# Transposes of the copied probabilities asked for two units later in each step, and the norm's power behind the normalisations on GpSimd

## The chip, the cores and the metric

The kernel runs on one core of one Trainium2 chip. A core has TensorE (PE, which loads its weights through a queue of its own, PEld), VectorE (DVE), ScalarE (ACT), GpSimd (POOL) and SyncE (SP, which here only issues transfers). Each engine works through its own queue in order; semaphores tell an engine that another one is done. The metric is the time of one launch in microseconds of device time, as the median of several runs. A profile is one further execution, recorded by the hardware profiler.

## What is computed

One layer of a hybrid backbone over 2048 latent tokens of width 1024, with 256 context tokens, all in fp32. From the reference, cut:

```python
h  = rms_norm(x) * (1 + scale) + shift
rq, rk, rv, rg, aq, ak, av, ag = project(h, w_in)
# group A: retention, 4 heads of 128, chunks of 128, forward and backward
y  = inner + cross                       # per chunk: (q k^T * decay) v, and q R * decay
y  = (y - mu) * rsqrt(var + EPS)         # per head
ret_x = y * gn_w * silu(rg)
# group B: attention, 8 heads of 64 (2 key heads), window +-128, 256 context keys, a sink
p  = exp(logits - m); p = p / (sum(p) + exp(sink - m))
att_x = (p[..., :Lc] @ v_ctx + p[..., Lc:] @ v_window) * silu(ag)
x  = x + gate * (concat(ret_x, att_x) @ w_out)
out = rms_norm(x) * final_norm_w
```

Products that must be near fp32 are made as three products of a high and a low part in fp32r (a x b high, high x low, low x high: `PASSES`).

## The kernel before

The first stage (to about 690 us in the profile) makes the normalised input and all its projections and puts queries, keys, values, gates and retention states in DRAM. The second stage, which the change concerns, works through 16 blocks of 128 tokens. A block b has two **steps**: t = 2b (kv = 0, an even step) and t = 2b + 1 (kv = 1, an odd step), one for each key head with its four query heads. Heads are prepared one step ahead: while step t multiplies probabilities with values, it makes the scores and probabilities for step t + 1.

What a step does is written as a row of **units**, in `STEPS[kv]`. A letter is a kind of work, the digit a part of it (the digits of a table's row and those of a tile's name are not the same):

- `a0`..`a3`: scores S of one head for the next step (four matmuls into the one PSUM tile S, L753 and L757), then VectorE adds the mask and takes the maximum (L759) and ScalarE takes the exponential (L768).
- `N0`..`N3`: the head's probabilities are normalised on GpSimd (L778, `p<-p`), then SP copies them (L782, `pr<-p`) into a second SBUF tile, from which TensorE may read them as fp32r.
- `T0`..`T4`: four transposes of the copied probabilities of one key tile (L1209, `pt<-identr,pr`), one for each head, into a PSUM bank; ScalarE takes the high part out (L1211, `phl`), VectorE the low part (L1212, `phl`).
- `V0`..`V4`: two matmuls with the values (L1222, `o`), one on the high and one on the low part.
- `o0`..`o7`: three matmuls each of the output projection (L1259, `pz`); `O`: the attention output of the step before (ACT `ob`, VectorE `mf`, GpSimd `ma`).
- Retention: `q` (decayed queries on GpSimd, L798, `qd`), `S` (scores `s`), `R` (the twelve products `y`, L813 to L815, and ScalarE's copy of them to `sd`), `B` (moments on VectorE), `r2` (the norm: GpSimd adds EPS and raises to -0.5, L119 and L120, `ra`; VectorE L832), `r0`, `r1` (two rows each of `sd` scaled on ScalarE, L839), `Y` (transposes `yt`; VectorE `gr` L1245; GpSimd `mr` L111 and L1248), `U` (VectorE's update of the state, L847, `st`, and the loads for the next blocks).
- `f`, `F0`, `F1`: the final norm of a finished block.

PSUM banks are short: S has one, `o` one, `pz` two, and `pt`, `y`, `s` and `yt` share three. The three `p` tiles in use rotate over all heads, and the copies of `phl` are two deep.

The row is what the kernel asks for. The framework that records the kernel then writes each engine's queue, and pulls an instruction ahead of others where it reckons with a wait. `with behind(i)` fixes that what stands inside comes after instruction i on its engine; the helper takes None for no such bond. The dictionary `PE` holds such instructions: `PE["norm"]` is the last normalisation recorded (L778), `PE["phl"]` the last high part. The retention norm has no such bond before the change; `qd` (L798) and the rows of `r0`, `r1` have one.

## Time and profile before

| what | us |
|---|---|
| median of 3 runs (lowest, highest) | 1181.89 (1181.22, 1182.31) |
| the profiled execution, its own time | 1180.44 |
| its span | 1178.7 |
| TensorE busy in the span | 1132.1 |
| first stage, 0 to 690: TensorE busy | 680.8 |
| second stage, one block in the middle | 30.0 |

The profiled execution lies 1.45 us below the median and 1.74 us above its own span. In a timeline a line gives the start, the length, the engine, the line of the code, the operation with output and inputs (without the buffers' numbers), the shapes, how many in a row, and in brackets the engine's idle time before it with what ended it. "PE busy" counts pipelined matmuls, so that it is nearly all of the time whenever no wait stands between them.

### The profile page before, as it was taken

How to read it: one execution, taken by the hardware profiler on the slowest of the kernel's cores; microseconds unless marked ns; L12 is line 12 of the kernel's file. 1: busy time of each engine (PE TensorE's matmuls, PEld its weight loads, DVE VectorE, ACT ScalarE, POOL GpSimd, SP SyncE). 2: the span in 40 equal slices, each digit the busy share in tenths (PEclk: the TensorE clock that was granted, in tenths of full speed). 3: DMA queues.
4: the chain of work that ended last, by engine and by line, in shares of the span. 5: the costliest groups of instructions: out<-in, count | busy, mean ns of one | idle time of the engine just before them, and what ended most of it. 6: DMA issues, size and time to landing. Idle time of an engine off the chain costs nothing. (4 is left out here: it accounts for less than half of the span.)

```text
span 1178.7 us, 18728 instructions
## 1 busy us (share of the span) xinstructions
PE 1132.1 (96%) x6317; PEld 966.0 (82%) x6318; DVE 796.4 (68%) x2028; ACT 476.7 (40%) x1032; POOL 323.3 (27%) x427
## 2 busy tenths in 40 slices
PE   8999999999999999999999987999999999999997
PEld 5887889999888899998888866788888888888885
DVE  7884974665557366475672656777777777777775
ACT  4445422343342022231111454555555555555553
POOL 0000020101002101011141523544444444455443
PEclk9998999999999999999999988999999999999999
DMA  9949982484575334353382674666666666666531
GB/s 332 348 124 288 297 290 68 152 269 147 177 248 170 90 117 135 94 166 107 90 270 91 188 250 149 223 208 220 210 216 217 217 217 213 214 210 214 181 123 72
DMA packets 158551, 224.38 MB, mean 190 GB/s; under 512 B 13299, under 2 KB 105203, under 8 KB 158326
## 3 DMA queue, kind: packets, MB, share of 16 engines
q1 hardware_dynamic: 143380, 215.54, 55.3%
q10 hardware_dynamic: 15074, 7.64, 2.2%
q8 instruction: 50, 0.82, 0.3%
q14 instruction: 47, 0.39, 0.1%
HBM read 130.19 MB, written 50.86 MB: 154 GB/s over the span
## 5 line engine op out<-in xcount | busy, mean ns | idle before, releaser
L768 ACT ACTIVATE p<-p,m 128x641 f32<-128x641 f32 (+1 forms) x128 | 105.0, 820 | 100.4 <-DVE m L765 55.9
L778 POOL TENSOR_SCALAR p<-p,m 128x640 f32<-128x640 f32 (+1 forms) x128 | 101.3, 795 | 104.5 <-DVE m L777 60.1
L1212 DVE TENSOR_TENSOR phl<-pt,phl 128x512 fp32r<-128x512 f32 x156 | 106.5, 685 | 33.8 <-ACT phl L1211 32.8
L759 DVE CUSTOM_DVE_ANT_0 p<-S,msk 128x640 f32<-128x640 f32 (+1 forms) x128 | 102.6, 802 | 31.5 <-PE S L757 9.4
L1211 ACT ACTIVATE phl<-pt 128x512 fp32r<-128x512 f32 x156 | 91.2, 595 | 65.7 <-PE pt L1209 60.4
L1259 PE MATMUL pz<-wg0h,mr 128*128 128x512 f32 x256 | 100.3, 407 | 1.2 <-DVE mr L115 1.0
L1259 PE MATMUL pz<-wg1h,ma 128*128 128x512 f32 x256 | 100.1, 409 | 0.1
L1209 PEld LDWEIGHTS pt<-identr,pr 128*128 128x128 f32 x624 | 70.1, 141 | 34.5 <-DMA pr<-p 23.0
L1209 PE MATMUL pt<-identr,pr 128*128 128x128 f32 x624 | 76.3, 241 | 22.2 <-DMA pr<-p 20.0
L753 PE MATMUL S<-kwin,aq 128*128 128x384 f32 (+1 forms) x256 | 84.2, 349 | 8.0 <-DVE p L764 5.0
L445 ACT ACTIVATE vw<-v,wdec 128x128 fp32r<-128x128 f32 x128 | 43.7, 394 | 84.3 <-DVE v L458 84.3
L1222 PE MATMUL o<-phl,vwin 128*128 128x512 f32 x184 | 70.7, 445 | 2.0 <-DVE phl L1212 1.5
L757 PE MATMUL S<-kctx,aq 128*128 128x256 f32 x256 | 72.0, 284 | 0.0
L753 PEld LDWEIGHTS S<-kwin,aq 128*128 128x128 f32 x256 | 49.0, 191 | 14.5 <-DVE m L759 6.2
L1259 PEld LDWEIGHTS pz<-wg0h,mr 128*128 128x128 f32 x256 | 48.6, 190 | 11.2 <-DVE mr L115 1.3
L1259 PEld LDWEIGHTS pz<-wg1h,ma 128*128 128x128 f32 x256 | 47.9, 188 | 8.3 <-POOL ma L1237 0.8
L757 PEld LDWEIGHTS S<-kctx,aq 128*128 128x128 f32 x256 | 49.3, 193 | 4.4
L1259 PE MATMUL pz<-wg0l,mr 128*128 128x512 f32 x128 | 51.0, 398 | 0.0
L1259 PE MATMUL pz<-wg1l,ma 128*128 128x512 f32 x128 | 50.4, 393 | 0.0
L1233 DVE TENSOR_TENSOR mf<-o,ob 64x256 f32<-64x256 f32 x64 | 26.5, 414 | 27.0 <-ACT ob L1230 26.3
L447 DVE SCALAR_TENSOR_TENSOR vw<-v,wdec,vw 128x128 fp32r<-128x128 f32 x128 | 40.0, 358 | 6.7 <-ACT vw L445 6.7
L1222 PEld LDWEIGHTS o<-phl,vwin 128*128 128x128 f32 x184 | 33.0, 193 | 12.5 <-ACT phl L1211 4.5
(425 smaller groups left out, 3037.2 us busy)
## 6 DMA issues: line engine op xcount, KB each, us to landing
pr<-p SPq DMA_DIRECT2D x112, 320.0 KB, 3.2
wss<-in_wss SPq DMA_DIRECT2D x32, 512.0 KB, 6.4
qkv<-d_qkv SPq DMA_DIRECT2D x15, 768.0 KB, 7.1
aq<-d_aq SPq DMA_DIRECT2D x64, 128.0 KB, 2.8
xb<-in_xn SPq DMA_DIRECT2D x16, 512.0 KB, 4.9
out<-xb SPq DMA_DIRECT2D x31, 256.0 KB, 2.6
st<-d_st SPq DMA_DIRECT2D x15, 512.0 KB, 3.4
d_g<-g ACTq DMA_DIRECT2D x28, 256.0 KB, 2.8
```

The costliest lines, as they stand in the source:

```text
L445: act.activation(vw[0][:, hh, dr, :], x, AF.Copy, scale=w)
L447: dve.scalar_tensor_tensor(vw[1][:, hh, dr, :], x, w, vw[0][:, hh, dr, :], op0=ALU.mult, op1=ALU.subtract)
L753: i = pe.matmul(psc[:, o:512].rearrange("p (s t) -> p s t", t=P), AQ[b][:, h, :], C2["kwin"][:, kv, hl, ksel], start=(hl == 0), stop=(hl = ...
L757: pe.matmul(psc[:, 512:768], AQ[b][:, h, :], C2["kctx"][:, kv, hl], start=(hl == 0), stop=(hl == 1))
L759: i = dve.tensor_tensor_reduce(out=pb[:, 0:n], in0=psc[:, o : o + n], in1=mk, op0=ALU.add, op1=ALU.max, scale=1.0, scalar=-3e38, accum_out ...
L768: act.activation(pb[:, 0 : n + 1], pb[:, 0 : n + 1], AF.Exp, bias=m4[:, 1, j : j + 1], scale=0.125, accum_out=m4[:, 2, j : j + 1],)
L778: PE["norm"] = pool.tensor_scalar(pb[:, 0:n], pb[:, 0:n], m4[:, 2, j : j + 1], 0.0, op0=ALU.mult, op1=ALU.add)
L1209: pe.transpose(ppt[:, j].bitcast(F32R), pb[:, j, kt * P : (kt + 1) * P], identr)
L1211: PE["phl"] = act.activation(phl[:, 0], ppt, AF.Copy)
L1212: PE["low"] = dve.tensor_tensor(phl[:, 1], ppt, phl[:, 0], op=ALU.subtract)
L1222: pe.matmul(PO[kv], vt, PH[kt][:, hl], start=(kt == 0 and hl == 0), stop=(kt == nkt - 1 and hl == 1))
L1259: pe.matmul(PZ[n2], m[:, a, k % RH, :], WG[k // 4][c][:, k % 4, s], start=(k == 0 and i == 0), stop=(k == NK - 1 and i == 2),)
```

## The change

Three things change. In both rows of `STEPS` the transposes T0 stand two units later (in the even step behind `a1 N0 o2` instead of directly behind `o1`, in the odd step behind `a1 N0 R`), most of the other T and V follow them more closely, and `r2` of the odd step comes behind `N3`. T0 is bound to stand on TensorE behind the last product recorded before it, of the projection or of y. And the norm's sum and power on GpSimd are bound to stand behind the last normalisation recorded.

```diff
 STEPS = (
-    "a0 o0 O o1 T0 r0 a1 N0 T1 r1 o2 V0 U a2 N1 T2 o3 Y V1 o4 a3 N2 T3 o5 V2 q o6 T4 N3 o7 V3 S f V4",
-    "a0 o0 O o1 T0 a1 N0 T1 R F0 F1 V0 a2 N1 T2 B V1 o2 a3 N2 T3 o3 V2 o4 T4 r2 N3 o5 V3 o6 V4 o7",
+    "a0 o0 O o1 a1 N0 o2 T0 r0 T1 r1 U a2 N1 V0 o3 T2 Y V1 o4 a3 N2 T3 V2 o5 q T4 N3 o6 V3 S o7 f V4",
+    "a0 o0 O o1 a1 N0 R T0 F0 F1 a2 N1 T1 B V0 o2 T2 V1 a3 N2 o3 T3 o4 V2 T4 N3 r2 o5 V3 o6 o7 V4",
 )
...
-            pe.matmul(py[:, h], sd[:, h], v[:, h], start=False, stop=True)
+            PE["prod"] = pe.matmul(py[:, h], sd[:, h], v[:, h], start=False, stop=True)
...
-        rs = inv_sqrt(ra[:, 0], mv[:, :, 1], 1)
+        with behind(PE["norm"] if b else None):
+            rs = inv_sqrt(ra[:, 0], mv[:, :, 1], 1)
...
-        for j in range(4):
-            pe.transpose(ppt[:, j].bitcast(F32R), pb[:, j, kt * P : (kt + 1) * P], identr)
+
+        with behind(PE.get("prod") if kt == 0 else None):
+            for j in range(4):
+                pe.transpose(ppt[:, j].bitcast(F32R), pb[:, j, kt * P : (kt + 1) * P], identr)
...
-            pe.matmul(
+            PE["prod"] = pe.matmul(
                 PZ[n2], m[:, a, k % RH, :], WG[k // 4][c][:, k % 4, s],
```

The queues show what this does in the middle blocks. On TensorE, in the odd step of block 7, the names carry block, key head and key tile: `pt7_1_0` is the tile of T0, `S8_1` the scores of the second head for block 8, `y8` the products of block 8. Before:

```order
L1209 MATMUL pt7_1_0_9106<-identr_71,pr7_1_8884 128x128 x3
L753 MATMUL S8_1_9114<-kwin_5977,aq8_8701 128x384
L757 MATMUL S8_1_9114<-kctx_5989,aq8_8701 128x256
L753 MATMUL S8_1_9114<-kwin_5977,aq8_8701 128x384
L757 MATMUL S8_1_9114<-kctx_5989,aq8_8701 128x256
L1209 MATMUL pt7_1_1_9126<-identr_71,pr7_1_8884 128x128 x3
L1209 MATMUL pt7_1_0_9106<-identr_71,pr7_1_8884 128x128
L1209 MATMUL pt7_1_1_9126<-identr_71,pr7_1_8884 128x128
L813 MATMUL y8_9134<-st7_8590,qd8_9022 128x128
```

Now, at the same place, from the end of the second scores on (eleven of the twelve y stand between; the first is ahead of the scores):

```order
L757 MATMUL S8_1_9106<-kctx_5989,aq8_8701 128x256
L814 MATMUL y8_9118<-st8_8952,qd8_9022 128x128
L815 MATMUL y8_9118<-qkv8_8517,sd8_9023 128x128
L813 MATMUL y8_9118<-st7_8587,qd8_9022 128x128
...
L814 MATMUL y8_9118<-st8_8952,qd8_9022 128x128
L815 MATMUL y8_9118<-qkv8_8517,sd8_9023 128x128
L1212 MATMUL pt7_1_0_9132<-identr_71,pr7_1_8884 128x128 x4
L753 MATMUL S8_2_9144<-kwin_5977,aq8_8701 128x384
```

T0, whose fourth transpose needs the copy of the fourth head, has moved from ahead of the products y to behind them.

On GpSimd, in the same odd step: `p8_0_1` to `p8_0_3` are the normalisations of three heads for block 8, `ra8` the norm's sum and power, `ma7` the attention output. Before:

```order
L778 TENSOR_SCALAR p8_0_1_9078<-p8_0_1_9078,m48_0_9076 128x640
L119 TENSOR_SCALAR ra8_9185<-mv8_9176 128x4
L120 TENSOR_TENSOR ra8_9185<-ra8_9185,half4_86 128x4
L778 TENSOR_SCALAR p8_0_2_9079<-p8_0_2_9079,m48_0_9076 128x640
L778 TENSOR_SCALAR p8_0_3_9080<-p8_0_3_9080,m48_0_9076 128x640
```

Now:

```order
L778 TENSOR_SCALAR p8_0_1_9078<-p8_0_1_9078,m48_0_9076 128x640
L778 TENSOR_SCALAR p8_0_2_9079<-p8_0_2_9079,m48_0_9076 128x640
L778 TENSOR_SCALAR p8_0_3_9080<-p8_0_3_9080,m48_0_9076 128x640
L119 TENSOR_SCALAR ra8_9174<-mv8_9165 128x4
L120 TENSOR_TENSOR ra8_9174<-ra8_9174,half4_86 128x4
```

The two instructions of the norm have moved behind both normalisations.

On ScalarE, in the even step of block 8: `phl8_0_0` is the high part of T0's tile, `sd8` two rows of the retention, `p8_1_1` the exponential of the second head. Before:

```order
L768 ACTIVATE p8_1_0_9251,m48_1_9250<-p8_1_0_9251,m48_1_9250 128x641
L1211 ACTIVATE phl8_0_0_9283<-pt8_0_0_9278 128x512
L839 ACTIVATE sd8_9023<-sd8_9023,ra8_9185 128x128 x2
L1211 ACTIVATE phl8_0_1_9305<-pt8_0_1_9300 128x512
L768 ACTIVATE p8_1_1_9252,m48_1_9250<-p8_1_1_9252,m48_1_9250 128x641
L839 ACTIVATE sd8_9023<-sd8_9023,ra8_9185 128x128 x2
L1211 ACTIVATE phl8_0_2_9341<-pt8_0_2_9336 128x512
```

Now:

```order
L768 ACTIVATE p8_1_0_9251,m48_1_9250<-p8_1_0_9251,m48_1_9250 128x641
L1214 ACTIVATE phl8_0_0_9298<-pt8_0_0_9293 128x512
L768 ACTIVATE p8_1_1_9252,m48_1_9250<-p8_1_1_9252,m48_1_9250 128x641
L840 ACTIVATE sd8_9023<-sd8_9023,ra8_9174 128x128 x2
L1214 ACTIVATE phl8_0_1_9308<-pt8_0_1_9303 128x512
L840 ACTIVATE sd8_9023<-sd8_9023,ra8_9174 128x128 x2
L768 ACTIVATE p8_1_2_9253,m48_1_9250<-p8_1_2_9253,m48_1_9250 128x641
L1214 ACTIVATE phl8_0_2_9344<-pt8_0_2_9339 128x512
```

The exponential of the second head has moved from behind the second high part to directly behind the first, and that of the third head ahead of the third high part. The lines of the changed kernel are one higher from L832 on, three higher from L1211 on.

## Prediction

> **What bounds the kernel now.** I read the page first, then the time by stage, then the waits of TensorE, and last the timeline and the chain of one block.

> ```profile
> span 1178.7 us, 18728 instructions
> PE 1132.1 (96%) x6317; PEld 966.0 (82%) x6318; DVE 796.4 (68%) x2028; ACT 476.7 (40%) x1032; POOL 323.3 (27%) x427
> 956.00:986.00 30.00, 28.71 (x179) 24.95 (x178) 23.59 (x76) 17.48 (x37) 15.14 (x20) 1.00 0.63 210
> ```

> The third row is one block of the second stage (columns: stretch, length, then busy time of PE, PEld, DVE, ACT and POOL, the granted clock, the DMA share). PE works 28.71 of 30.00 us, no other engine over 23.6: PE is the bound, and only its idle 1.29 us a block are to be had. The longest of the waits of PE from 690 us on names them (total, times, longest):

> ```profile
> PE pt L1209 <- DMA pr<-p: 20.0, 19, 2.0
> ```

> These 20.0 us are the transposes waiting for the copied probabilities. By place:

> ```profile
> 769.61 0.36 PE L1209 MATMUL pt<-identr,pr 128*128 128x128 f32 x2 [1.28 <-DMA pr<-p]
> 1099.96 0.36 PE L1209 MATMUL pt<-identr,pr 128*128 128x128 f32 x2 [1.30 <-DMA pr<-p]
> 1129.52 0.28 PE L1209 MATMUL pt<-identr,pr 128*128 128x128 f32 x1 [1.96 <-DMA pr<-p]
> 753.77 0.28 PE L1209 MATMUL pt<-identr,pr 128*128 128x128 f32 x1 [0.48 <-DMA pr<-p]
> ```

> The first two are the first and last of 12, one in each odd step, 1.26 to 1.34 us each, 15.4 in all. The third is the last odd step with products behind it. The fourth is the longest of a few small ones in even steps; these and one wait in the first odd step make the remaining 20.0 - 15.4 - 2.0 = 2.6 us. The chain through one of the twelve:

> ```profile
> 970.85 0.62 POOL mr L111
> 972.83 0.80 POOL p L778
> 973.63 2.50 POOL qd L798 x2
> 976.13 0.79 POOL p L778
> 976.94 2.80 DMA pr<-p
> 979.78 0.36 PE pt L1209 x2
> ```

> GpSimd works without a pause from 970.85, the last normalisation stands behind the 2.5 us of `qd`, and its copy lands 2.8 us after that. PE was there 1.29 us before.

> **The transposes of an odd step.** The change puts T0 behind the state products y.

> ```profile
> 977.47 0.41 PE L753 MATMUL S<-kwin,aq 128*128 128x384 f32 x1
> 978.12 0.37 PE L1209 MATMUL pt<-identr,pr 128*128 128x128 f32 x3
> 979.98 0.46 PE L813 MATMUL y<-st,qd 128*128 128x128 f32 x2
> 982.65 0.71 PE L1222 MATMUL o<-phl,vwin 128*128 128x512 f32 x2
> 969.14 0.39 PE L1259 MATMUL pz<-wg1l,ma 128*128 128x512 f32 x1
> 969.37 0.40 PE L1259 MATMUL pz<-wg1h,ma 128*128 128x512 f32 x1
> 968.57 0.27 PE L1243 MATMUL yt<-ident,sd 128*128 128x128 f32 x1
> 970.08 0.68 DVE L1245 TENSOR_TENSOR gr<-yt,gr 128x512 f32<-128x512 f32 x1
> 967.44 1.14 DVE L847 SCALAR_TENSOR_TENSOR st<-st,gC,st 128x128 f32<-128x128 f32 x4
> ```

> All twelve products y take 982.65 - 979.98 = 2.67 us; in the new order eleven of them stand between the second scores and T0, so 2.45 us are added ahead of T0. Against that, three projection products of 0.23 us (969.37 - 969.14) now stand before the transposes `yt` instead of behind them, so the chain, which starts at `yt`, starts 0.7 us nearer to T0. PE so comes 2.45 - 0.7 - 1.29 = 0.46 us after the data, if `gr` follows `yt` as before. It should follow sooner: it started 970.08 - 968.84 = 1.24 us after the end of `yt`, behind other VectorE work, and now it stands straight behind the four `st` updates (1.14 us), which are ready earlier. I put that at 0.3 to 0.8 us after `yt`: margin 0.9 to 1.4 us, bounds 0.46 and 1.7. The twelve waits go, and so does the one in the first odd step.

> **The transposes of an even step.** T0 moves behind the second scores (978.12 - 977.47 = 0.65 us for a set) and three projection products (0.69), 1.34 us. The power moves as well:

> ```profile
> 987.76 0.25 POOL L119 TENSOR_SCALAR ra<-mv 128x4 f32<-128x4 f32 x1 [3.54 <-DVE p L764]
> 989.12 1.58 POOL L778 TENSOR_SCALAR p<-p,m 128x640 f32<-128x640 f32 x2
> ```

> Both normalisations (x2) stood behind the sum and the power of the norm, 989.12 - 987.76 = 1.36 us, and sent their copies one behind the other; now each goes when it is ready. Earlier data and later transposes cover small waits of at most 0.5 us. What the power itself now delays is the factor for the rows `sd`, which ScalarE needs only after the next T0, and VectorE's short operation on it (L832), with `mf` and the reduction of the next scores queued behind. `mf` waits for the last `o` of the step anyhow, and that hides it; without this cover it would cost up to the 1.36 us a block. I take nothing in the middle blocks. In the first block, where PE waits for VectorE already, the power can cost up to its 1.36 us once; I take 0.5. SP issues the same copies, only `pr` before `st` and `qkv`: nothing.

> **The last long wait and the clock.**

> ```profile
> 1133.00:1134.00 1.00, 1.00 (x7) 1.00 (x7) 0.41 (x2) 0.00 (x0) 0.49 (x1) 0.50 0.04 16
> 1130.48 0.45 PE L813 MATMUL y<-st,qd 128*128 128x128 f32 x2
> 1134.78 0.71 PE L1222 MATMUL o<-phl,vwin 128*128 128x512 f32 x2
> ```

> After the 1.96 us the granted clock (third figure from the end) is 0.50 and the same products take 1134.78 - 1130.48 = 4.30 us, 1.63 more than at 980 us. After a wait of 1.29 us it stays at 1.00 (the row of the block). I count the 1.63 with the wait. [...]

> **What comes late next.** In the even step T0 now stands closer to V0, and ScalarE has the exponential of the second head ahead of the first rows. One block's ScalarE before, and below it the transposes of one tile, a reduction of scores and the exponential that follows from it:

> ```profile
> 964.95 0.60 ACT L1211 ACTIVATE phl<-pt 128x512 fp32r<-128x512 f32 x1
> 965.45 0.87 ACT L839 ACTIVATE sd<-sd,ra 128x128 f32<-128x128 f32 x2
> 966.22 0.58 ACT L1211 ACTIVATE phl<-pt 128x512 fp32r<-128x512 f32 x1
> 966.70 0.82 ACT L768 ACTIVATE p<-p,m 128x641 f32<-128x641 f32 x1
> 967.51 0.87 ACT L839 ACTIVATE sd<-sd,ra 128x128 f32<-128x128 f32 x2
> 968.28 0.58 ACT L1211 ACTIVATE phl<-pt 128x512 fp32r<-128x512 f32 x1
> 967.12 0.29 PE pt L1209 x4
> 968.49 0.82 DVE L759 CUSTOM_DVE_ANT_0 p<-S,msk 128x640 f32<-128x640 f32 x1
> 969.65 0.84 ACT L768 ACTIVATE p<-p,m 128x641 f32<-128x641 f32 x1 [0.79 <-issue]
> ```

> From start to start a phl costs 0.49, two rows 0.77, an exponential 0.81. The new row phl, p, sd, phl, sd, p, phl takes 0.49 + 0.81 + 0.77 + 0.49 + 0.77 + 0.81 + 0.58 = 4.7 us up to what V2 needs. PE has between T0 and V2 the transposes T1, T2, T3 (0.29 each, 0.9), two sets of scores (1.3), four products o and six pz (ten of 0.23, 2.3) and `yt` (four more transposes, 0.3): 4.8 us. The margin is 0.1 us at V2, and I put it at about -0.1 at V0, at V1 and at the third scores, whose bank VectorE must read first. That makes 0.3 us in an even step, and about 0.1 in an odd one, where the copy of y now stands ahead of the first phl. Before, the even step had small waits of its own, about 0.2 us, which go. 0.3 + 0.1 - 0.2 = 0.2 us a block, and 0.1 for hand-offs that I have not followed: I take 0.3, between -0.2 (the old ones go, none comes) and 0.8, times 14: 4.2 us (-3 to 11).

> **Sum.** 20.0 + 1.6 - 4.2 - 0.5 = 16.9 us. The profiled execution took 1180.44 us, so 1163.5; the median of the runs shown is 1181.89, 1.45 above it, and what is measured is compared with that: **1165 us**.

> **Rivals.**
> 1. *The wait stays in part.* The chain starts with `gr`; if VectorE takes it up some 1.6 us later than I think, beyond the margin of 0.9, 0.7 us of each 1.29 stay.

> ```profile
> 736.23 1.32 DVE L1235 TENSOR_TENSOR mf<-mf,ga 128x256 f32<-128x256 f32 x1
> 734.72 2.54 POOL L798 TENSOR_TENSOR qd<-qkv,decq 128x512 f32<-128x512 f32 x2
> 963.38 0.41 DVE L1235 TENSOR_TENSOR mf<-mf,ga 128x256 f32<-128x256 f32 x1
> ```

> For it: the same operation took 1.32 instead of 0.41 us while GpSimd worked on `qd`, so the `st` updates ahead of `gr` may be held up beside a normalisation (0.80), and `gr` queues behind two more VectorE operations if the order of arrival is unkind. [...] Against it: the normalisation before should be over by then. Time: 13 x 0.7 = 9.1 less gain, about 1174. Chance 0.16.

> 2. *ScalarE's row in the even step becomes the bound: slower.* The exponential stands ahead of both pairs of rows and all three phl; it waits for VectorE's reduction of scores issued only just before T0. Each us that it is late, less the 0.1, is a PE wait in every block. The gain is 21.6 - 0.5 over 14 blocks, 1.5 us a block, so it decides from 1.6 us late on; at 2.1 us late, 14 x 2.0 = 28 us, less the 21.1, the time is 1189. Against it: an exponential begins 969.65 - 968.49 = 1.16 us after its reduction starts, which puts it within 0.1 us of the end of the first phl. Chance 0.09.

> 3. *Gains and new waits cancel.* 1.5 us a block of many small hand-offs between PE, ScalarE and VectorE with PSUM banks reused sooner: 1182. Chance 0.05.

> The forecast has the remaining 0.70, its own range 1158 (old small waits gone, no new ones) to 1171 (0.8 a block).

> **Range and chances.** A tenth is left out on either side at most: 1158 is everything gained and nothing lost; the high end takes in the first rival, 1175. What a measurement of this kernel can tell from no change is about 0.2%, 2.4 us. Faster: forecast and first rival, 0.86; same: 0.05; slower: 0.09.

> **What would show it.** In the changed profile the wait of `pt` on the copies should be under 3 us in all, the block 28.7 to 29.1 us, the clock 1.00 at 1110 to 1130 us. New waits of PE should read o <- ACT phl and S <- DVE m, each about 0.1 to 0.2 us. GpSimd's power should stand behind the fourth normalisation with no engine waiting for it. Wrong it would be if `pt` still waited over 0.5 us in the odd steps (first rival), or if o or yt waited for ACT over 1 us in the even ones (second).

## The result, and the profile after

The changed kernel takes **1165.01 us** (median of four runs, 1162.25 to 1165.74), the kernel before on the same chip 1181.66 us. The ratio is 0.9854, with a 95% interval of 0.9837 to 0.9871: faster by 16.65 us, where the prediction had 1165 and 16.9. The profiled execution of the changed kernel took 1164.85 us with a span of 1163.1.

First the page's head, then one block of the second stage as the time by stage gives it (stretch, length, busy time of PE, PEld, DVE, ACT and POOL, granted clock, DMA share, GB/s):

```profile
span 1163.1 us, 18715 instructions
PE 1128.2 (97%) x6317; PEld 963.0 (83%) x6318; DVE 793.8 (68%) x2028; ACT 470.0 (40%) x1032; POOL 332.8 (29%) x427
948.10:976.73 28.63, 28.39 (x178) 24.74 (x177) 23.35 (x76) 16.84 (x36) 16.00 (x20) 1.00 0.66 225
```

A block takes 28.63 instead of 29.95 us, and PE idles 0.24 us of it instead of 1.29. What the longest waits of PE from 690 us on name, and three places in the timeline:

```profile
PE S L753 <- DVE p L764: 5.2, 2, 5.0
PE o L1225 <- ACT phl L1214: 3.9, 14, 0.6
PE pt L1212 <- DMA pr<-p: 1.3, 3, 0.8
974.64 0.54 PE L1212 MATMUL pt<-identr,pr 128*128 128x128 f32 x4
976.37 0.50 PE L1225 MATMUL o<-phl,vwin 128*128 128x512 f32 x1 [0.24 <-ACT phl L1214]
1119.40 0.50 PE L1225 MATMUL o<-phl,vwin 128*128 128x512 f32 x1 [0.56 <-ACT phl L1214]
```

The transposes' wait for the copied probabilities has gone from 20.0 to 1.3 us; T0 of the odd step (974.64) has no bracket, so it did not wait. In its place stands one new wait of 0.24 us in every odd step: the first product with the values waits for ScalarE's high part. In the even steps of the middle blocks nothing new appears. The wait of 1.96 us in the last odd step is gone, and 0.56 us for a high part stands there (1119.40).

To see where the span's 15.6 us came from, I cut both executions at the first product of the retention scores (`s`, L805) of blocks 0, 3 and 15. Of these cuts, before (blocks 0, 3, 15) and after (blocks 0, 3, 15):

```profile
668.22 0.83 PE L805 MATMUL s<-first 128*128 128x128 f32 x6
763.79 1.05 PE L805 MATMUL s<-qkv 128*128 128x128 f32 x8
1123.99 1.05 PE L805 MATMUL s<-qkv 128*128 128x128 f32 x8
```

```profile
671.77 0.83 PE L805 MATMUL s<-first 128*128 128x128 f32 x6
765.80 0.39 PE L805 MATMUL s<-qkv 128*128 128x128 f32 x2
1110.25 0.38 PE L805 MATMUL s<-qkv 128*128 128x128 f32 x2
```

The twelve blocks between the last two cuts take 360.2 us before and 344.5 after: 15.7, or 1.31 us a block. The stretch up to block 3 gains 1.6 (95.6 to 94.0) and the end 1.9 (54.7 to 52.9). In these two, 0.9 us is work that only changed sides: in the new even row four products of 0.23 us (a projection unit and one product with the values) stand behind the products `s` instead of ahead of them. Without that, the stretch up to block 3 gains 0.6 and the end 2.8. Up to the first cut the changed kernel's execution is 3.6 us behind; the change touches nothing there. A part of it is a stretch in which the granted clock was 0.50 in one execution alone (one row of before and one of after, the same 3.4 us); there the lag of PE's products grows from 1.0 to 2.5 us. The rest is not placed:

```profile
236.10:239.50 3.40, 3.40 (x31) 3.40 (x30) 3.40 (x7) 1.14 (x4) 0.00 (x0) 1.00 0.56 161
```

```profile
236.10:239.50 3.40, 3.40 (x18) 3.40 (x18) 3.25 (x5) 0.12 (x1) 0.00 (x0) 0.50 0.27 46
```

### The profile page after: what moved, and what is told of

It is laid out like the page before. It is cut to its first block, busy times and chain, and to the rows that moved or that the text cites. A ratio compares the mean times of both kernels' runs of the same rounds, so it can differ in the third digit from the quotient of the medians.

```text
span 1163.1 us, 18715 instructions
## 1 busy us (share of the span) xinstructions
PE 1128.2 (97%) x6317; PEld 963.0 (83%) x6318; DVE 793.8 (68%) x2028; ACT 470.0 (40%) x1032; POOL 332.8 (29%) x427
## 5 line engine op out<-in xcount | busy, mean ns | idle before, releaser
L768 ACT ACTIVATE p<-p,m 128x641 f32<-128x641 f32 (+1 forms) x128 | 104.6, 817 | 91.7 <-DVE m L765 49.4
L778 POOL TENSOR_SCALAR p<-p,m 128x640 f32<-128x640 f32 (+1 forms) x128 | 106.9, 837 | 115.5 <-DVE m L777 73.5
L1215 DVE TENSOR_TENSOR phl<-pt,phl 128x512 fp32r<-128x512 f32 x156 | 106.8, 686 | 23.6 <-ACT phl L1214 22.2
L759 DVE CUSTOM_DVE_ANT_0 p<-S,msk 128x640 f32<-128x640 f32 (+1 forms) x128 | 102.3, 799 | 9.5 <-PE S L757 5.1
L1262 PE MATMUL pz<-wg0h,mr 128*128 128x512 f32 x256 | 97.3, 403 | 1.6 <-DVE mr L115 1.6
L753 PE MATMUL S<-kwin,aq 128*128 128x384 f32 (+1 forms) x256 | 86.9, 359 | 7.2 <-DVE p L764 5.2
L1212 PEld LDWEIGHTS pt<-identr,pr 128*128 128x128 f32 x624 | 69.2, 142 | 16.9 <-DVE glast L1191 2.6
L1225 PE MATMUL o<-phl,vwin 128*128 128x512 f32 x184 | 75.1, 438 | 5.2 <-ACT phl L1214 3.9
L1212 PE MATMUL pt<-identr,pr 128*128 128x128 f32 x624 | 73.2, 244 | 3.6 <-DVE glast L1191 2.2
L753 PEld LDWEIGHTS S<-kwin,aq 128*128 128x128 f32 x256 | 49.1, 192 | 13.3 <-issue 5.4
L1225 PE MATMUL o<-phl,vctx 128*128 128x512 f32 x128 | 44.8, 410 | 0.3 <-DVE phl L1215 0.2
```

What stands on the lines that cost most here:

```text
L753: i = pe.matmul(psc[:, o:512].rearrange("p (s t) -> p s t", t=P), AQ[b][:, h, :], C2["kwin"][:, kv, hl, ksel], start=(hl == 0), stop=(hl = ...
L759: i = dve.tensor_tensor_reduce(out=pb[:, 0:n], in0=psc[:, o : o + n], in1=mk, op0=ALU.add, op1=ALU.max, scale=1.0, scalar=-3e38, accum_out ...
L768: act.activation(pb[:, 0 : n + 1], pb[:, 0 : n + 1], AF.Exp, bias=m4[:, 1, j : j + 1], scale=0.125, accum_out=m4[:, 2, j : j + 1],)
L778: PE["norm"] = pool.tensor_scalar(pb[:, 0:n], pb[:, 0:n], m4[:, 2, j : j + 1], 0.0, op0=ALU.mult, op1=ALU.add)
L1212: pe.transpose(ppt[:, j].bitcast(F32R), pb[:, j, kt * P : (kt + 1) * P], identr)
L1215: PE["low"] = dve.tensor_tensor(phl[:, 1], ppt, phl[:, 0], op=ALU.subtract)
```

## The experiments

The theory under test is the prediction's: PE reached the odd step's T0 1.28 us ahead of the fourth copy, and putting T0 behind the products y covers that; the even step's row and the power's bond matter little. The first rival is that another part of the change carries the gain. Each kernel was compared with runs of the kernel before on the same chip, whose medians lie between 1181.66 and 1182.29 us; the ratios go by these. "Block" is a twelfth of the stretch between the cuts of blocks 3 and 15 in the profiled execution.

| kernel | median, us | ratio to before (95%) | block, us |
|---|---|---|---|
| before | 1181.66 | 1 | 30.02 |
| changed | 1165.01 | 0.9854 (0.9837 to 0.9871) | 28.70 |
| rows, without the power's bond | 1165.28 | 0.9854 (0.9834 to 0.9873) | 28.88 |
| power's bond alone | 1184.15 | 1.0019 (1.0008 to 1.0029) | 30.42 |
| even row alone | 1185.80 | 1.0029 (1.0017 to 1.0041) | 30.02 |
| odd row alone | 1188.88 | 1.0055 (1.0041 to 1.0069) | 30.61 |
| odd row, final norm behind the attention output | 1163.01 | 0.9842 (0.9825 to 0.9859) | 29.07 |
| changed, copy 1.27 us later | 1181.82 | 0.9997 (0.9983 to 1.0011) | 30.08 |
| changed, first V later | 1165.39 | 0.9855 (0.9838 to 0.9871) | 28.84 |
| changed, final norm behind the reduction | 1158.35 | 0.9806 (0.9792 to 0.9819) | 28.76 |
| odd row, final norm behind the reduction | 1159.65 | 0.9815 (0.9800 to 0.9830) | 28.80 |
| before, final norm behind the reduction | 1177.69 | 0.9968 (0.9957 to 0.9979) | 30.00 |
| copy 1.27 us later, final norm behind the reduction | 1167.47 | 0.9877 (0.9861 to 0.9893) | 29.07 |

### The parts of the change, one at a time

**Without the power's bond** (the changed kernel, the norm as before):

```diff
-        with behind(PE["norm"] if b else None):
-            rs = inv_sqrt(ra[:, 0], mv[:, :, 1], 1)
+        rs = inv_sqrt(ra[:, 0], mv[:, :, 1], 1)
```

> The changed rows and the bond of T0 stay; the bond of the norm's power is taken out, so that the power stands ahead of the fourth normalisation of the odd step again (sum and power took 1.36 us in the trace of before). My theory: the fourth copy comes up to 1.36 us later, and the transposes of the even step, which now stand two sets of work (1.34 us) later, still come about in time: the same as the changed kernel, 1165, at most 3 us above it. Rival: the bond is what frees the even step's data, and the transposes wait again, 0.5 us or more in each of 14 blocks: 1172 or above.

**The power's bond alone** (the kernel before, with these two lines put in):

> The kernel before with nothing but the bond of the norm's power. My theory: the odd step's waits on the fourth copy (12 of 1.28 us and one of 1.96 us) hang on the normalisation behind the decayed queries, which the power does not touch: 1180 to 1182, at most the small waits of the even steps (about 1.3 us in all) gone. Rival: the order on GpSimd was the cause of the waits, and the bond alone brings a third or more of the gain: 1176 or less.

**The even row alone**: the odd row, `STEPS[1]`, as before; T0 bound in even steps only; y and the projection's products in odd steps bound behind the last transposes, which keeps PE's order of before there. The power's bond stays, in this kernel and in every one below that is made from the changed kernel.

```diff
-        with behind(PE.get("prod") if kt == 0 else None):
+        with behind(PE.get("prod") if kt == 0 and kv == 0 else None):
```

> The changed row and bond of T0 for the even step alone; the odd step has its old row, and further bonds hold the products of the state and of the projection behind its transposes, as before. The power's bond stays. My theory: the odd step's waits of 1.28 us stay, and 1179 to 1182 is left. Rival: the even step's new order takes the chain ahead of the odd step's data forward as well, by half of the wait or more: 1172 or less.

**The odd row alone**: `STEPS[0]` as before, and T0 bound in odd steps only.

```diff
-        with behind(PE.get("prod") if kt == 0 else None):
+        with behind(PE.get("prod") if kt == 0 and kv == 1 else None):
```

> The changed row and bond of T0 for the odd step alone; the even step has its old row. The power's bond stays. My theory: the gain lies in the odd step, 15.4 us in its twelve waits, 1.3 in the first odd step and 2 to 3.6 at the last long wait: 1164 to 1168. Rival: the even step's later transposes carry a good part of the gain, because in its old row the transposes or V0 wait 0.3 us or more a block: 1170 or above.

The first came as expected: without the bond the time is the same, and the wait for the copies is 2.9 us in all. The power alone gains nothing (1184.15, slightly above the 1180 to 1182 expected); its odd steps wait as before. The even row alone brings nothing either (1185.80, over the 1179 to 1182 expected): its undisturbed blocks take 29.8 us, 0.15 under those of before, but its profiled execution lost more elsewhere, among it 58.0 us from block 15 on instead of 54.7. One row of PE's waits from each of these three:

```profile
PE pt L1212 <- DMA pr<-p: 2.9, 4, 1.0
```

```profile
PE pt L1210 <- DMA pr<-p: 22.5, 19, 1.9
```

```profile
PE pt L1213 <- DMA pr<-p: 18.8, 18, 1.6
```

The odd row alone, where I had put the gain, is the **slowest of all, 1188.88 instead of 1164 to 1168**. So the account was short of something. Its waits, and VectorE and PE at one odd step:

```profile
PE S L753 <- DVE m L759: 17.0, 13, 2.1
PE pt L1212 <- DMA pr<-p: 2.1, 4, 0.8
```

```profile
954.82 0.58 POOL L120 TENSOR_TENSOR rz<-rz,half 128x1 f32<-128x1 f32 x1
955.43 0.75 DVE L1286 SCALAR_TENSOR_TENSOR xb<-xb,rz,fw 128x512 f32<-128x512 f32 x1 [1.71 <-POOL rz L120]
956.10 0.82 DVE L759 CUSTOM_DVE_ANT_0 p<-S,msk 128x640 f32<-128x640 f32 x1
956.98 0.44 PE L753 MATMUL S<-kwin,aq 128*128 128x384 f32 x1 [1.30 <-DVE m L759]
```

The wait for the copies has gone there as the theory says (2.1 us). But VectorE's final norm of the last block (L1286) now stands ahead of the reduction of the first head's scores (L759). It waits 1.71 us for its factor `rz`, which GpSimd makes behind the last normalisation; the reduction waits behind it, and the second scores need the bank that the reduction reads: 1.30 us of PE, in each odd step. The queues show that it was the framework that pulled the final norm forward. VectorE in the odd step of block 7 of this kernel (`xb6` is block 6's result, `mf7_0` the attention output):

```
L1286 SCALAR_TENSOR_TENSOR xb6_8342<-xb6_8342,rz6_9055,fw_6429 128x512
L759 ISA p8_0_0_9077,m48_0_9076<-S8_0_9081,msk_6005 128x640
...
L1236 TENSOR_TENSOR mf7_0_9097<-o7_0_8948,ob7_0_9095 64x256
```

In the changed kernel the final norm stands behind the attention output, after that reduction. That is a new theory: the odd row gives the gain, and the even row serves only to leave VectorE's order harmless. The next kernel tests it.

### The final norm held back

**The odd row alone, with the final norm behind the attention output:**

```diff
-        dve.tensor_tensor(mf, mf, GA[b][:, ks], op=ALU.mult)
+        PE["mf"] = dve.tensor_tensor(mf, mf, GA[b][:, ks], op=ALU.mult)
...
-        dve.scalar_tensor_tensor(x, x, RZ[b], fw[:, n * GT : (n + 1) * GT], op0=ALU.mult, op1=ALU.mult)
+        with behind(PE["mf"]):
+            dve.scalar_tensor_tensor(x, x, RZ[b], fw[:, n * GT : (n + 1) * GT], op0=ALU.mult, op1=ALU.mult)
```

> The kernel with the odd step's row alone, which took 1188.9 us, and one more bond: the final norm's first half stands on VectorE behind the attention output, as in the changed kernel, and not ahead of the reduction of the next head's first scores. My theory: the wait of 1.30 us a block (second scores, for VectorE's reduction, which stood behind a final norm that waited 1.71 us for GpSimd) goes, and what the odd row saves is left: a block of 28.6 to 29.0 us, 1165 to 1169 in all. Rival: the wait hangs on something else in the old even row (the last product with the values comes later), and stays, 0.5 us a block or more: 1176 or above.

It took 1163.01 us, under the 1165 to 1169 expected: the 1.30 us waits are gone and the whole gain is there, without the even row. The block, 29.07, is just over the 28.6 to 29.0 expected; the rest came earlier. From the cut of block 0 to that of block 3 this kernel takes 90.4 us and the changed one 94.0; the longest wait of PE there, near 722 us, is 1.73 instead of 5.03 us.

**The first product with the values one unit later** in the changed kernel's odd row:

```diff
-    "a0 o0 O o1 a1 N0 R T0 F0 F1 a2 N1 T1 B V0 o2 T2 V1 a3 N2 o3 T3 o4 V2 T4 N3 r2 o5 V3 o6 o7 V4",
+    "a0 o0 O o1 a1 N0 R T0 F0 F1 a2 N1 T1 B o2 V0 T2 V1 a3 N2 o3 T3 o4 V2 T4 N3 r2 o5 V3 o6 o7 V4",
```

> The changed kernel with the first product with the values one unit later in the odd step, behind three products of the projection (0.69 us). My theory: the wait of 0.24 us for ScalarE's high part, which comes in every odd step behind its copy of y, goes, 0.24 x 13 = 3.1 us: 1161 to 1163. Rival: the wait only moves, to the next transposes or products with the values, since the high parts are two deep and the bank of the transposes comes free later: 1165.

The waits of 0.24 us went, yet the time is 1165.39. Its undisturbed blocks shrink by under 0.1 us (28.55), and three even steps wait 1.15, 0.45 and 0.99 us for a copy. The expectation of 1161 to 1163 failed, and the rival's time, 1165, came. What makes the 0.24 us shows in the changed kernel itself:

```profile
971.73 0.58 POOL L120 TENSOR_TENSOR rz<-rz,half 128x1 f32<-128x1 f32 x1
972.46 0.75 DVE L1286 SCALAR_TENSOR_TENSOR xb<-xb,rz,fw 128x512 f32<-128x512 f32 x1
973.12 0.82 DVE L759 CUSTOM_DVE_ANT_0 p<-S,msk 128x640 f32<-128x640 f32 x1
974.28 0.83 ACT L768 ACTIVATE p<-p,m 128x641 f32<-128x641 f32 x1 [1.06 <-POOL ma L1240]
975.23 0.60 ACT L817 ACTIVATE sd<-y 128x512 f32<-128x512 f32 x1
975.72 1.10 ACT L1214 ACTIVATE phl<-pt 128x512 fp32r<-128x512 f32 x2
```

Here too the final norm stands ahead of a reduction, now that of the second head: final norm, reduction, exponential, copy of y, high part, and PE at 976.37. The factor is ready at 972.31 and the final norm starts without an idle time of VectorE before it, so what stands in the way in this block is the 0.66 us from its start to that of the reduction. The bracket of the exponential names GpSimd's `ma`; in the kernel with the next bond the exponential of the same head starts before `ma` ends (966.22 and 966.35 us), so it does not wait for it. **Both instructions of the final norm behind that reduction:**

```diff
+        PE["red"] = i
         with behind(i):
             dve.tensor_copy(pb[:, n : n + 1], sink8[:, h : h + 1])
...
-        dve.scalar_tensor_tensor(x, x, RZ[b], fw[:, n * GT : (n + 1) * GT], op0=ALU.mult, op1=ALU.mult)
+        with behind(PE["red"]):
+            dve.scalar_tensor_tensor(x, x, RZ[b], fw[:, n * GT : (n + 1) * GT], op0=ALU.mult, op1=ALU.mult)
```

Here `i` is the reduction just recorded. This bond went into the changed kernel, into the odd row alone and into the kernel before:

> The changed kernel with the final norm's two instructions on VectorE bound behind the reduction of the second head's scores of the same step. My theory: the wait of 0.24 us in each odd step hangs on GpSimd's factor of the final norm (VectorE's final norm waits for it, the reduction behind it, the exponential, ScalarE's copy of y and the high part behind that), and the single wait of 5.03 us at 723 us on the same queue; both go, 0.24 x 13 = 3.1 us and about 5: 1155 to 1160. Rival: as with the product moved later, the short waits are no loss, and the early one only moves: 1162 to 1166.

> The odd step's row alone with this same bond of the final norm. My theory: all of the change's gain is the odd step's T0; the even step's row adds 0.1 to 0.2 us a block: within 3 us of the kernel with both rows and this bond, 1155 to 1163. Rival: the even step's row is needed for more than the order on VectorE: 1168 or above.

> The kernel before with nothing but this bond of the final norm. My theory: the twelve waits of 1.28 us on the copies stay, the early wait of some 5 us goes in good part: 1175 to 1179. Rival: the final norm's place is what holds the odd steps in the kernel before as well: 1170 or less.

All three came as the theory had it: 1158.35, 1159.65 and 1177.69. With the bond the times of the two kernels with the odd row cannot be told apart, so the even row is worth nothing that the times can measure. The power's bond is in both of them; what speaks for its being worth nothing is the changed kernel without it (1165.28). The odd row, together with the power's bond, is worth 18 us (1177.69 to 1159.65). One block of the changed kernel with the final norm's bond, the same of the odd row alone with it, and one of the waits of PE left in the first:

```profile
938.00:966.35 28.35, 28.35 (x179) 24.78 (x178) 23.86 (x76) 16.85 (x36) 15.58 (x22) 1.00 0.66 227
938.00:966.72 28.72, 28.69 (x178) 24.84 (x177) 23.94 (x76) 17.01 (x36) 15.56 (x20) 1.00 0.64 224
895.18 0.62 PE L1213 MATMUL pt<-identr,pr 128*128 128x128 f32 x5 [1.26 <-DMA pr<-p]
888.71 6.42 DMA pr<-p
```

PE does not idle in the first block at all, and the early wait, at 716.26, is 1.41 instead of 5.03 us. An undisturbed block with both rows is 0.37 us shorter than with the odd row alone, since PE's work in it is less. But with both rows there are three even steps in which PE waits 1.1 to 1.3 us for the fourth copy (the row at 895.18 is one), and over the twelve blocks the two kernels come out alike (28.76 and 28.80). Against the changed kernel, the bond gains 3.6 us of the profile between the cuts of blocks 0 and 3 (94.0 to 90.4); the twelve blocks gain nothing, as the three late copies take back what the waits of 0.24 us had cost. The last row is from the chain of waits of the place at 895.18: this copy took 6.42 us from issue to landing, where that of the block before landed in 4.4; why some copies land late, these runs do not tell.

### The margin

**One half of the decayed queries made twice** (the same values are written again), in the changed kernel and in the one with the final norm behind the reduction:

```diff
             for dr in range(2):
                 pool.tensor_tensor(RT[b][0][:, dr], QKV[b][:, 0], C2["decq"][:, dr], op=ALU.mult)
+            if b > 1:
+                pool.tensor_tensor(RT[b][0][:, 1], QKV[b][:, 0], C2["decq"][:, 1], op=ALU.mult)
```

> The changed kernel with one half of the decayed queries made twice (the same values written again), so that the last normalisation of an even step and its copy come 1.27 us later. It measures the margin that the prediction put at 0.9 to 1.4 us, with a lower bound of 0.46. By that margin PE waits 0 to 0.4 us for the copy in each odd step: 1165 to 1170. Rival (the margin is at its lower bound or under it): 0.8 us or more in each of 13 odd steps, 1175 or above.

> The kernel whose GpSimd works 1.27 us longer ahead of the last normalisation, now with this bond of the final norm. My theory: there the 1.27 us reached PE through the final norm's factor, VectorE and ScalarE (about 1.0 us a block), and through the copies only in 0.15 us; with the bond, 0.15 to 0.4 us in each odd step are left, 2 to 5 us above the changed kernel with this bond: 1158 to 1165. Rival: they came by the later products y and the attention output: 1170 or above.

The first took 1181.82 us, far over the 1165 to 1170 expected, as if the margin were nothing. But a part of it alone is the copy's. From 690 us on PE waits 9.0 us in all for the copies (1.3 in the changed kernel) and 9.7 us for ScalarE's high part (3.9). An odd step of the first kernel in which the copy's part is small:

```profile
802.87 0.28 PE L1214 MATMUL pt<-identr,pr 128*128 128x128 f32 x1 [0.20 <-DMA pr<-p]
805.10 0.50 PE L1227 MATMUL o<-phl,vwin 128*128 128x512 f32 x1 [1.00 <-ACT phl L1216]
```

The 1.00 us is the second chain, through the final norm's factor, which stands behind the delayed normalisation. In the second kernel, with the final norm held back, those waits are gone, and the twelve waits for copies in odd steps that are left sum to 5.0 us, 0.15 to 0.92 each; one more odd step has none. So there the margin of the copy is 1.27 less these: 0.35 to 1.12 us, 0.86 in the mean. In the first kernel three odd steps wait 1.18, 1.21 and 2.46 us for a copy, so single steps have next to no margin there, or none. The second kernel stands 9.1 us above its own base, over the 2 to 5 expected; the two profiled executions are 6.5 us apart. Their rows give 5.0 in the odd steps and 2.2 for one early wait of the products y for the doubled work (2.65 us, of which 0.47 is there without it), and 1.7 less in the even steps; the rest is not placed.

### The clock

**Single waits of growing length**: in the changed kernel, one half of the decayed queries made again 1, 2, 3 and 4 times for blocks 5, 8, 11 and 14.

```diff
+            for _ in range({5: 1, 8: 2, 11: 3, 14: 4}.get(b, 0)):
+                pool.tensor_tensor(RT[b][0][:, 1], QKV[b][:, 0], C2["decq"][:, 1], op=ALU.mult)
```

> The changed kernel with one half of the decayed queries made again 1, 2, 3 and 4 times (1.27 us each) for blocks 5, 8, 11 and 14 alone. It makes single waits of PE of growing length. With a margin of 0.9 us they would be about 0.4, 1.6, 2.9 and 4.2 us. My theory of the clock: a wait of about 1.9 us or more is followed by a granted clock of 0.50 for some 3.4 us, so the third and fourth are, the first is not, and the second is open. [...]

The one run of this kernel took 1180.48 us. The waits of PE at blocks 8, 11 and 14:

```profile
920.51 0.28 PE L1214 MATMUL pt<-identr,pr 128*128 128x128 f32 x1 [2.29 <-DMA pr<-p]
1008.01 0.49 PE L816 MATMUL y<-st,qd 128*128 128x128 f32 x2 [2.78 <-POOL qd L800]
1100.22 0.80 PE L816 MATMUL y<-st,qd 128*128 128x128 f32 x2 [4.11 <-POOL qd L800]
```

The granted clock is 0.50 from 921.23 us on, behind the first, and from 1098.72 us on, within the third, and it **stays at 1.00 behind the second**, which is longer than the first (rows below). So in this execution the length of the wait does not decide, and my theory fell. The two drops lie 177.49 us apart, 52 times 3.413 us. In the execution of the kernel before, the six stretches at 0.50 ahead of the one at the end begin at 8.02, 100.19, 683.86, 690.69, 718.00 and 1131.01 us, the last five 27, 198, 200, 208 and 329 times 3.413 us after the first, and they last 1, 2, 1, 1, 3 and 1 times as long. Cut into pieces of that length, with borders at the two drops, the graded kernel reads:

```profile
917.81:921.23 3.42, 1.13 (x10) 0.99 (x10) 2.58 (x10) 1.86 (x4) 3.00 (x3) 1.00 0.59 167
921.23:924.64 3.41, 3.41 (x16) 2.92 (x15) 2.96 (x14) 1.78 (x4) 0.11 (x1) 0.50 0.91 345
1003.15:1006.56 3.41, 2.08 (x12) 1.60 (x10) 2.87 (x7) 1.90 (x4) 3.33 (x3) 1.00 0.15 44
1006.56:1009.97 3.41, 1.96 (x17) 1.96 (x18) 0.99 (x2) 0.00 (x0) 3.15 (x6) 1.00 0.60 178
1009.97:1013.38 3.41, 2.35 (x21) 2.17 (x21) 2.57 (x10) 2.41 (x5) 2.61 (x3) 1.00 0.13 39
1095.31:1098.72 3.41, 0.79 (x6) 0.52 (x5) 1.59 (x3) 0.92 (x2) 3.35 (x3) 1.00 0.02 5
1098.72:1102.13 3.41, 1.91 (x9) 1.92 (x10) 0.95 (x2) 0.00 (x0) 3.08 (x6) 0.50 0.72 211
```

PE was busy 1.13 and 0.79 us of the pieces that a drop follows. The wait of 2.78 us lies across two pieces and leaves 2.08 and 1.96 us of work in them; no drop follows. The kernel before, and the one with the copy 1.27 us later, tighten this from both sides:

```profile
1127.60:1131.01 3.41, 1.49 (x14) 1.49 (x15) 1.89 (x6) 1.49 (x4) 1.59 (x3) 1.00 0.45 173
1131.01:1134.42 3.41, 3.41 (x19) 3.41 (x18) 2.40 (x9) 1.15 (x3) 1.38 (x2) 0.50 0.14 50
```

```profile
738.50:741.91 3.41, 1.62 (x14) 1.62 (x15) 1.08 (x4) 0.00 (x0) 3.41 (x5) 1.00 0.44 138
741.91:745.33 3.42, 3.42 (x26) 2.92 (x26) 1.65 (x7) 2.29 (x5) 0.31 (x2) 1.00 0.64 249
```

In these rows 1.49 us of work in a piece is followed by a granted clock of 0.50, and 1.62 us is not. This is no boundary that holds everywhere. Two pieces of the changed kernel with the final norm behind the reduction, one behind the other, and the piece ahead of the drop at 236 us in the changed kernel:

```profile
714.38:717.79 3.41, 1.78 (x15) 1.44 (x13) 2.06 (x7) 1.96 (x4) 0.93 (x3) 1.00 0.78 321
717.79:721.20 3.41, 1.60 (x5) 1.20 (x5) 1.76 (x8) 0.88 (x2) 1.96 (x3) 0.50 0.32 115
232.70:236.10 3.40, 3.40 (x17) 2.02 (x17) 0.00 (x0) 2.64 (x4) 0.00 (x0) 1.00 0.90 355
```

Here 1.78 us is followed by a drop, and the drop at 236 us comes behind a piece in which the profile has PE busy throughout. So in these executions PE's busy time in a piece does not by itself say whether the next one is at 0.50.

## Why the prediction was right, step by step

- **The bound.** PE's idle 1.29 us a block were what was to be had: the block fell by 1.32, from 29.95 to 28.63.
- **The odd step's T0.** Right, and shown: the waits of the odd steps go in every kernel that has the odd row and no added delay, and stay in every kernel without it. The step that the margin rests on came too: `gr` was to start 0.3 to 0.8 us after the end of `yt` and starts 0.45 us after it, straight behind the four `st` updates (rows of the changed kernel below). The margin, put at 0.9 to 1.4 us with a bound of 0.46, measures 0.86 in the mean and 0.35 at the least, in the kernel with the final norm held back: the estimate was at its edge, the bound slightly too high. The first rival, that the wait stays in part, did not come.

```profile
963.46 0.27 PE L1246 MATMUL yt<-ident,sd 128*128 128x128 f32 x1
964.18 0.68 DVE L1248 TENSOR_TENSOR gr<-yt,gr 128x512 f32<-128x512 f32 x1
```

- **The even step and the power.** Both counted at nothing in the middle blocks, and nothing is what the times measure; that with both rows an undisturbed block is 0.37 us shorter than with the odd row alone was not foreseen. The 0.5 us for the first block did not show: the early waits of 5.03 and about 1 us are there before and after. The products y wait 1.6 us in all for the decayed queries in the first blocks of the changed kernel, but 1.1 us in the kernel before with the final norm's bond as well, so these runs do not put that down to the power.
- **The last wait and the clock.** 3.6 us were counted. The end gained 1.9 by the cuts; with the 0.9 of work that now stands in it and the new wait of 0.56, some 3.3 is what the removal gave. That the clock's drop belonged to the wait agrees with the changed kernel, where the wait is gone and the granted clock is 1.00 from 734.46 to 1161.13 us. The reason given, that 1.96 us is long enough and 1.29 is not, was wrong: a wait of 2.78 us had no drop behind it. That it counts as well how a wait lies in the pieces of 3.413 us is my estimate from the work in them: 1.49 us in the piece ahead of the drop at 1131.01 us, but 2.08 and 1.96 us in the two across the wait of 2.78.
- **New small waits: the mis-sized term.** Put at 0.3 us a block net, 4.2 in all. Measured: 0.24 in the odd step, none in the even one, and PE's own work in the block 0.27 lower (28.66 to 28.39), so that the block fell by a little more than the removed wait; with the odd row alone it is not lower (28.69), so it takes both rows, and why, the rows do not tell. The odd step's was foreseen as ScalarE's copy of y ahead of the first high part, 0.1 us. The copy does stand there, but it comes late through the final norm on VectorE; with the final norm held back, the wait is gone.
- **The sum.** From the first cut on, the span gained 19.1 us where 16.9 were forecast, mainly because the 4.2 us of new waits came to nothing net; the 3.6 us of the first stage, which differ between executions, brought it back to 15.6 in the profiles. That the median came within 0.3 us, 16.65, is therefore in part luck.
- **What was missed.** The prediction followed the order on PE, GpSimd and ScalarE. VectorE's order, which the rows also set, was the real danger: with the odd row alone, one waiting final norm ahead of one reduction cost all of the gain and 7 us more. The second rival named ScalarE's even step as the place that could turn the sign; for the odd row alone the place was VectorE's odd step. In the changed kernel it costs 0.24 us a block, and there a good part of the 1.27 us of delay tried on GpSimd went through it.

## What to carry to other kernels

When a step is moved to cover a wait, look at every in-order queue for an instruction that waits for something else and has come to stand ahead of what the critical engine needs; here a final norm of no urgency decided between 1189 and 1163 us. Test a part of a change alone, but read its queues first: a part can be slower than nothing for a reason that the whole does not have. The best version found here is the changed kernel with the final norm behind the second head's reduction, 1158.35 us; the odd row alone with it, 1159.65, cannot be told from it.
